# Two-layer hybrid encoder: weight halves three parts ahead, raw weights in three buffers, moves at three per part

## The chip, the core and the metric

The kernel runs on one core of a Trainium2 chip. The metric is the device time of one execution in microseconds (us). A core has a matrix engine (TensorE, PE in the profile; its weight loads are PEld), a vector engine (VectorE, DVE), a scalar engine (ScalarE, ACT), GpSimd (POOL) and SyncE (SP), which here only issues transfers from main memory. The engines run in parallel, each one in the order of its own queue, and wait for each other by semaphores. SBUF is the on-chip working memory; PSUM holds what PE sums up.

## The reference

The input is 256 tokens of 2048 channels, in float32. Each of two layers does this:

```python
h = rms_norm(x, norm_g)
u = jnp.einsum('bsd,de->bse', h, w_in)               # q, k, v, gate path of four mixers, merge gates
ya, yb, yc, yd = four attention mixers of u            # A, B, C, D; 4 heads of 128 each
y = jnp.stack([ya, yb, yc, yd], axis=2)
z = jnp.stack([az, bz, cz, dz], axis=2)
branch = jnp.einsum('bsnm,nmd->bsnd', y * jax.nn.silu(z), w_branch)
gate = jax.nn.sigmoid(gates.reshape(b, s, N_BRANCH, D_MODEL) + gate_b)
merged = jnp.sum(gate * branch, axis=2)
x = x + jnp.einsum('bsd,de->bse', merged, w_out)
```

and the output is a last `rms_norm` of `x`. All weights are float32.

## The kernel before

**Parts.** All weight matrices of both layers are one list of 640 tiles of 128 x 1024 float32 (512 KB each). What the program does with one tile is called a part here; `j` counts the parts. To keep float32 accuracy, a weight tile `raw` is split into two halves of a shorter format: `whi` is `raw` rounded (ACT, line 286), and `wlo` is `raw` minus `whi` (DVE, line 287). The activations are split in the same way. A part is 12 matmuls of 512 columns: for each of two row tiles of the weights and two blocks of 128 tokens, high by high, high by low and low by high (lines 213 to 215; `mm3`, `mm_m`). In the program's names the first and third line of each three read `whi`, the second reads `wlo`.

**Lookahead.** In part `j` the loop (from line 668) issues the load of tile `j + LD` (`LD` = 4, `dma_w`, line 112), splits tile `j + LS` (`LS` = 2, `split_w`, line 119) and issues the matmuls of tile `j`. There are four `raw` buffers and three each of `whi` and `wlo`. So the split of tile `j + 2` writes the buffers of tile `j - 1` and waits until PE has finished part `j - 1`; and a load waits until the tile that was in its buffer has been split, on ACT and on DVE. In the first parts the input `x` comes in eight pieces (`dma_x`, `h_tiles`), and the loads of weights 1 to 3 stand ahead of the loop, held back by small copies on POOL (`hold`).

**Units.** Parts form units: `M` (8 parts, one block of columns of the input projection), `G` (8 parts, a gate), `R` (2 parts, a branch projection) and `P` (8 parts, the output projection), in the order of `unit_list` (line 45). When a unit is done, its result is taken out of PSUM by DVE and ACT (`ev_M`, `ev_gate`, `ev_branch`, `ev_out`). PSUM has two buffers for units.

**Moves.** Results that the next product needs the other way round are turned (`turn`, line 300): one DVE transpose within 32 x 32 blocks (line 312), then 16 ACT copies that move the blocks (line 314, "moves" here), then a split into halves. The moves do not stand in one piece: they go to a list `post`, `step` of them in each following part, behind that part's split (`issue_after`, line 718). The step is 3 for most turns, 4 for branch D and 6 for the merged branches (`ev_branch`, for `x == "B"`, line 567) and for the second layer's input (`ev_out`, line 584). The order in a queue is made by a scheduler that sees these constraints, so two neighbouring groups of moves may end up side by side.

**Attention.** The attention of a branch is cut into steps `s1` to `s7` (line 406) that run in slots between the parts. `s5` splits the transposed probabilities of a head into `pth` and `ptl` (two buffers each), and `s6` multiplies them on PE.

**The end.** In the last unit (`alone`) the two blocks of tokens have PSUM buffers of their own. From `si >= 5` on only block 0 is multiplied at once; block 1's products of those parts (`late`) follow after the last part, so that block 0 can be finished and written out (`ev_last`) beside them.

Of the kernel before, what the change touches and what calls it, by code (L numbers as in the profile page):

```python
# [9 lines left out]
F32 = mybir.dt.float32  # L10
F32R = mybir.dt.float32r
# [6 lines left out]
P = 128  # L18
SEQ = 256
# [55 lines left out]
def encoder_kernel(ctx: ExitStack, tc: tile.TileContext, a: dict, out: bass.AP):  # L75
    nc = tc.nc
    LD = 4
    LS = 2
    NBUSY = 10

    const = ctx.enter_context(tc.tile_pool(name="const", bufs=1))
# [2 lines left out]
    wpool = ctx.enter_context(tc.tile_pool(name="wpool", bufs=4))  # L84
    wk = ctx.enter_context(tc.tile_pool(name="wk", bufs=2))
# [7 lines left out]
    def nm(s):  # L93
        uid[0] += 1
        return f"{s}_{uid[0]}"
# [8 lines left out]
    raw_q = {}  # L104
# [6 lines left out]

    def dma_w(j, after=None):
        if j < NSUB:
            t = wpool.tile([P, 1024], F32, tag="raw", name=nm("raw"))
            hold(t, after)
            nc.sync.dma_start(t, a["w"][j])
            raw_q[j] = t

    def split_w(j):
        if j < NSUB:  # L120
            raw = raw_q.pop(j)
            hi = wpool.tile([P, 1024], F32R, tag="whi", name=nm("whi"), bufs=3)
            lo = wpool.tile([P, 1024], F32R, tag="wlo", name=nm("wlo"), bufs=3)
            for c in (slice(0, 512), slice(512, 1024)) if j == 0 else (slice(0, 1024),):
                last = halves(raw[:, c], hi[:, c], lo[:, c])
            wstate[j] = (hi, lo)
            return last
        return None
# [5 lines left out]
    xT = {0: x0[:, NV:].rearrange("p (k t) -> p k t", k=2)}  # L134
    xm = [per.tile([P, 2, 512], F32, name=f"xm{n}") for n in range(4)]

    def dma_x(i, after=None):
        if 0 < i < 8:
            xT[i] = st()[:, 0:2, :]
            hold(xT[i][:, 0, :], after)  # L140
            nc.sync.dma_start(xT[i], a["x"][:, 2 * i:2 * i + 2, :])

    nc.sync.dma_start(x0, a["x0"])
    raw_q[0] = wpool.tile([P, 1024], F32, tag="raw", name=nm("raw"))
    for q in range(2):
        c = slice(q * 512, (q + 1) * 512)
        nc.sync.dma_start(raw_q[0][:, c], a["w"][0][:, c])
# [1 line left out]
    dma_x(1, raw_q[0][:, 0:1])  # L149
    dma_w(2, raw_q[0][:, 512:513])  # L150
    dma_x(2, raw_q[1][:, 0:1])
    dma_w(3, xT[1][:, 0, 0:1])
    assert LD == 4
    ones = const.tile([P, P], F32, name="ones")
    nc.vector.memset(ones, 1.0)
    warm = const.tile([P, 1], F32, name="warm")
# [163 lines left out]
    def turn_split(u, tmp, hi, lo, post, step=3):  # L320
        t = tmp.rearrange("p (h t) -> p h t", t=SEQ)
        turn(u, t, post, lambda: halves(t, hi, lo), step)
# [83 lines left out]
    def attn_slots(x, layer):  # L406
# [79 lines left out]
                nc.tensor.transpose(H[h][:, k, blk * P:(blk + 1) * P], it["p"][:, k * P:(k + 1) * P], ident)  # L486

        def s5(h):
            hi = wk.tile([P, 2, SEQ], F32R, tag="pth", name=nm("pth"))
            lo = wk.tile([P, 2, SEQ], F32R, tag="ptl", name=nm("ptl"))  # L490
            halves(H.pop(h), hi, lo)
            H[h] = hi, lo

# [60 lines left out]
    def ev_branch(x, n, ps, post):  # L554
        G = S.pop("G")
        if x == "A":
            S[f"m{n}"] = per.tile([P, 2, 512], F32, tag=f"m{n}", name=nm("m"))
        m = S[f"m{n}"]
        for blk in range(2):
            o = m if x == "A" else G  # L560
            nc.vector.tensor_tensor(o[:, blk, :], ps[:, blk, :], G[:, blk, :], op=ALU.mult)  # L561
        if x != "A":
            nc.vector.tensor_tensor(m, m, G, op=ALU.add)  # L563
        if x == "B":

            S[f"mh{n}"], S[f"ml{n}"] = st(F32R), st(F32R)
            turn_split(m, m.rearrange("p b m -> p (b m)"), S[f"mh{n}"], S[f"ml{n}"], post, 6)

    def ev_out(n, ps, post):

        nc.vector.tensor_tensor(xm[n], ps, xm[n], op=ALU.add)
        for blk in range(2):
            s = squares(F["ss"], n, blk)
        if n == 0:
            sqrt_table(s[:, 0:1])

        h_tile(n)
        t = wk.tile([P, 4, SEQ], F32, tag="u", name=nm("u"), bufs=1)

        def split():  # L580
            for c in range(4):
                h_split(1, 4 * n + c, t[:, c, :])

        turn(xm[n], t, post, split, 6)

    F = {}

# [44 lines left out]
    def h_tiles(i):  # L632
        if i < 8:
            for c in range(2):
                h_split(0, 2 * i + c, xT[i][:, c, :])
# [28 lines left out]
    for layer in range(DEPTH):  # L664
        final = layer + 1 == DEPTH
        units = unit_list(layer)
        opened = {}
        for ui, si in sub_list(layer):
            kind, name, i = units[ui]
            nsub = unit_subs(kind)  # L670
            alone = final and (kind, i) == ("P", 3)
            if si == 0:
                if kind == "G":
                    b = BR.index(name)
                    gb = wk.tile([P, 512], F32, tag="gb", name=nm("gb"), bufs=1)
                    if (layer, name, i) == (0, "A", 0):
                        hold(gb, xm[3][:, 0, 0:1])
                    nc.sync.dma_start(gb, a["gate_b"][layer, b:b + 1, i * 512:(i + 1) * 512].partition_broadcast(P))
                    S["gb"] = gb
                if name == "bk":  # L680
                    b_bias(layer)
                if (kind, i) == ("P", 0):
                    new_sums()
                    if final:
                        fin_start()
                ps = ps_main.tile([P, 2, 512], F32, tag="main", name=nm("ps"))
                outs = [(blk, ps[:, blk, :]) for blk in range(2)]
                if alone:
                    outs[1] = 1, ps_main.tile([P, 2, 512], F32, tag="main", name=nm("ps"))[:, 1, :]
                if kind == "R":  # L690
                    yh, yl = S[name + "yh"], S[name + "yl"]
                    sh, sl = (lambda k: yh[:, k, :]), (lambda k: yl[:, k, :])
                elif kind == "P":
                    sh, sl = (lambda k, h=h: S[f"m{h}{k // 4}"][:, k % 4, :] for h in "hl")
                else:
                    sh, sl = (lambda k, h=h: hs[k // 4][:, h, k % 4, :] for h in range(2))
                opened[ui] = ps, outs, sh, sl
            ps, outs, sh, sl = opened[ui]
            nk = 2 * nsub
            if (name, si) in (("akdk", 5), ("dq", 5)):  # L700
                d_tables(layer, int(name == "akdk"), None if layer or name == "dq" else xm[3][:, 0, 0:1])
            dma_x(j + LD - 1)
            dma_w(j + LD)
            h_tiles(j + LS - 1)
            behind = split_w(j + LS)
            if j in early:
                early[j]()
            if j == 11:
                layer_stats(0, F["ss"])
                ev_M(*held.pop())  # L710
            hi, lo = wstate.pop(j)
            half = alone and si >= 5
            mm_m(outs[:1] if half else outs, hi, lo, sh, sl, 2 * si, nk, j < 4)
            if half:
                late.append((hi, lo, si))
            with ExitStack() as order:
                for ins in behind or ():
                    order.enter_context(tc.issue_after(ins.ins))
                for f in post[:1]:
                    f()  # L720
                del post[:1]
                if si == nsub - 1:
                    if kind == "M" and "rc" not in S:
                        held.append((layer, name, ps, post))
                    elif kind == "M":
                        ev_M(layer, name, ps, post)
                    elif kind == "G":
                        ev_gate(layer, name, i, ps)
                    elif kind == "R":
                        ev_branch(name, i, ps, post)  # L730
                    elif not final:
                        ev_out(i, ps, post)
                        if i == 3:
                            layer_stats(1, F["ss"])
                    else:
                        ev_last(i, 0, outs[0][1])
                        for h, l, s in late:
                            mm_m(outs[1:], h, l, sh, sl, 2 * s, nk)
                        ev_last(i, 1, outs[1][1])
                    if kind == "M" and name[1:] == "z":  # L740
                        x = name[0].upper()
                        for k, s in enumerate(attn_slots(x, layer)):
                            side.append(s)
                            side.extend([] for _ in range(SPREAD[x][k % 2]))
                if side:
                    for fn, arg in side.pop(0):
                        fn(arg)
            j += 1
        assert final or not side
# [120 lines left out]
```

## Time and profile before

| what | value |
|---|---|
| median of 3 runs | 1863.76 us (1863.42 to 1864.97) |
| the profiled execution | 1864.2 us, of which the span of the profile is 1862.4 us |
| PE busy | 1833.5 us, 98% of the span |
| PEld busy | 1505.5 us, 81% |
| DVE busy | 1179.0 us, 63% |
| ACT busy | 1151.7 us, 62% |
| `wlo` split, DVE, x641 | 1220 ns each |
| `whi` split, ACT, x641 | 1058 ns each |
| loads of `raw`, x639 | 512 KB each, 3.9 us to landing (median) |
| DMA | 192 GB/s on average |

The span is cut into 40 slices on the page; PE shows 9 or more tenths in all but the last, and the clock granted to it is 9 tenths or more in all. The record of a 512-column matmul is about 0.39 us long, but the records overlap: a matmul starts before the record of the one before it ends. For what PE loses, the distance from start to start is therefore read, and not the busy share.

### The profile page before, as it was taken

The page shows a single profiled execution, that of the slowest core. Times are in us where ns is not written, and L with a number is a line of the kernel's source. Part 1 is how long each engine was busy: PE and PEld are TensorE (multiplying, and loading weights), DVE is VectorE, ACT ScalarE, POOL GpSimd, SP SyncE. Part 2 cuts the span into 40 slices and gives each one's busy share as a digit, 9 for nine tenths or more (in the row PEclk, how much of TensorE's full clock was granted, in tenths as well). Part 3 has the DMA queues.
Part 4 walks back from the last instruction along what each step waited for, and adds up shares of the span by engine and source line. Part 5 has one row for each costly group of instructions (what it writes and reads, how often), then busy time and mean ns, then how long its engine had stood idle before and what let it go on. Part 6 is the DMA issues. An engine that isn't in the chain of part 4 may idle for free.

```text
span 1862.4 us, 22697 instructions
## 1 busy us (share of the span) xinstructions
PE 1833.5 (98%) x8260; PEld 1505.5 (81%) x8260; DVE 1179.0 (63%) x1600; ACT 1151.7 (62%) x1712; POOL 5.1 (0%) x18
## 2 busy tenths in 40 slices
PE   9999999999999999999999999999999999999998
PEld 7888788888888888777888887888888888887776
DVE  6767566666665675665557675765666556755655
ACT  6676666556446764667767676655575457546663
POOL 1000000000000000000000000000000000000000
PEclk9999999999999999999999999999999999999999
DMA  8655555665576566655665555566655765565754
GB/s 310 203 184 181 180 178 188 198 196 175 183 208 204 180 189 195 197 186 174 190 204 186 177 172 180 175 207 198 196 175 175 220 198 178 189 199 180 222 190 148
DMA packets 110848, 356.94 MB, mean 192 GB/s; under 512 B 19984, under 2 KB 20496, under 8 KB 110736
## 3 DMA queue, kind: packets, MB, share of 16 engines
q1 hardware_dynamic: 110448, 354.98, 60.2%
q8 instruction: 64, 1.05, 0.2%
q10 hardware_dynamic: 288, 0.52, 0.1%
q14 instruction: 48, 0.39, 0.1%
HBM read 353.36 MB, written 2.10 MB: 191 GB/s over the span
## 4 chain that ended last, share of the span: by engine, by line
PE 84%; ACT 9%; DVE 4%; issue 2%; DMA 1%; POOL 0%; DVEq 0%; SPq 0%; ACTq 0%; POOLq 0%
PE ps L214 27%; PE ps L215 27%; PE ps L213 26%; ACT whi L286 2%; DVE wlo L287 2%; ACT u L314 2%; ACT m L314 2%; ACT st L314 1%; PE tp L486 1%; DVE T L312 1%; DVE m L563 0%; ACT dku L314 0%; DMA raw<-w 0%; PE y L214 0%; PE y L213 0%
## 5 line engine op out<-in xcount | busy, mean ns | idle before, releaser
L287 DVE TENSOR_TENSOR wlo<-raw,whi 128x1024 fp32r<-128x1024 f32 (+1 forms) x641 | 779.7, 1220 | 612.1 <-ACT whi L286 609.6
L286 ACT ACTIVATE whi<-raw 128x1024 fp32r<-128x1024 f32 (+1 forms) x641 | 676.4, 1058 | 606.7 <-PE ps L215 486.0
L214 PE MATMUL ps<-wlo,h 128*128 128x512 f32 x2032 | 794.9, 391 | 10.1 <-DVE wlo L287 9.3
L213 PE MATMUL ps<-whi,h 128*128 128x512 f32 x2032 | 794.5, 391 | 2.1 <-ACT whi L286 2.1
L215 PE MATMUL ps<-whi,h 128*128 128x512 f32 x2032 | 791.7, 390 | 0.0
L214 PEld LDWEIGHTS ps<-wlo,h 128*128 128x128 f32 x2032 | 381.7, 188 | 95.6 <-DVE wlo L287 20.7
L213 PEld LDWEIGHTS ps<-whi,h 128*128 128x128 f32 x2032 | 381.7, 188 | 82.4 <-ACT whi L286 5.5
L215 PEld LDWEIGHTS ps<-whi,h 128*128 128x128 f32 x2032 | 381.6, 188 | 78.8
L214 PE MATMUL ps<-wlo,st 128*128 128x512 f32 x512 | 200.8, 392 | 4.6 <-DVE wlo L287 4.6
L213 PE MATMUL ps<-whi,st 128*128 128x512 f32 x512 | 199.8, 391 | 2.2 <-ACT whi L286 2.2
L215 PE MATMUL ps<-whi,st 128*128 128x512 f32 x512 | 199.3, 389 | 0.0
L214 PEld LDWEIGHTS ps<-wlo,st 128*128 128x128 f32 x512 | 96.1, 188 | 28.4 <-DVE wlo L287 8.9
L213 PEld LDWEIGHTS ps<-whi,st 128*128 128x128 f32 x512 | 96.1, 188 | 24.0 <-ACT whi L286 3.9
L215 PEld LDWEIGHTS ps<-whi,st 128*128 128x128 f32 x512 | 96.2, 188 | 19.4
L314 ACT ACTIVATE st<-T 32x256 f32<-32x256 f32 x256 | 106.2, 415 | 7.8 <-DVE T L312 4.1
L314 ACT ACTIVATE u<-T 32x256 f32<-32x256 f32 (+1 forms) x224 | 89.5, 399 | 7.2 <-DVE T L312 4.3
L314 ACT ACTIVATE m<-T 32x256 f32<-32x256 f32 x128 | 53.2, 415 | 10.2 <-DVE T L312 8.7
L549 DVE SCALAR_TENSOR_TENSOR G<-ps,ry,gb 128x512 f32<-128x512 f32 x64 | 45.0, 745 | 12.9 <-PE ps L215 12.8
L551 ACT ACTIVATE G<-G 128x1024 f32<-128x1024 f32 x32 | 34.0, 1061 | 6.9 <-DVE G L549 6.8
L312 DVE STREAM_TRANSPOSE T<-u 128x1024 f32<-128x1024 f32 (+1 forms) x26 | 31.2, 1199 | 7.7 <-ACT dku L314 7.5
L561 DVE TENSOR_TENSOR G<-ps,G 128x512 f32<-128x512 f32 x48 | 30.9, 684 | 5.6 <-PE ps L215 5.6
L459 ACT ACTIVATE p<-p,ng 128x256 f32<-128x256 f32 (+1 forms) x48 | 27.6, 574 | 6.1 <-DVE ng L458 5.2
(141 smaller groups left out, 836.5 us busy)
## 6 DMA issues: line engine op xcount, KB each, us to landing
raw<-w SPq DMA_DIRECT2D x639, 512.0 KB, 3.9
gb<-gate_b SPq DMA_DIRECT2D x32, 256.0 KB, 4.4
xm<-xm SPq DMA_DIRECT2D x4, 512.0 KB, 8.9
st<-rpb SPq DMA_DIRECT2D x32, 64.0 KB, 4.2
st<-x SPq DMA_DIRECT2D x7, 256.0 KB, 6.2
dx<-tabx SPq DMA_DIRECT2D x4, 256.0 KB, 3.9
st<-fg SPq DMA_DIRECT2D x2, 512.0 KB, 5.3
out<-xm SPq DMA_DIRECT2D x4, 256.0 KB, 2.6
```

What stands on the lines that cost most here:

```text
L213: nc.tensor.matmul(o, ah, bh, start=start, stop=False)
L214: nc.tensor.matmul(o, ah, bl, start=False, stop=False)
L215: nc.tensor.matmul(o, al, bh, start=False, stop=stop)
L286: return (nc.scalar.activation(hi, u, AF.Copy), nc.vector.tensor_tensor(lo, u, f32(hi), op=ALU.subtract))
L287: nc.vector.tensor_tensor(lo, u, f32(hi), op=ALU.subtract))
L312: nc.vector.transpose(t, u)
L314: nc.scalar.activation(y[c:c + 32, :, :, a:a + 32], x[a:a + 32, :, :, c:c + 32], AF.Copy)
L459: nc.scalar.activation(p[:, 0:n], p[:, 0:n], AF.Exp, bias=ng, scale=1.0, accum_out=den)
L486: nc.tensor.transpose(H[h][:, k, blk * P:(blk + 1) * P], it["p"][:, k * P:(k + 1) * P], ident)
L549: nc.vector.scalar_tensor_tensor(G[:, blk, :], ps[:, blk, :], S["rc"][:, blk:blk + 1], gb, op0=ALU.mult, op1=ALU.add)
L551: nc.scalar.activation(G, G, AF.Sigmoid)
L561: nc.vector.tensor_tensor(o[:, blk, :], ps[:, blk, :], G[:, blk, :], op=ALU.mult)
```

## The change

- `LS` becomes 3: in part `j` tile `j + 3` is split; `whi` and `wlo` have four buffers each (the pool's default). The split of tile `j + 3` then again writes the buffers of tile `j - 1`.
- `raw` has three buffers in place of four. The load of tile `j + 4` writes the buffer of tile `j + 1`, which is split in part `j - 2`.
- In the first parts the older distances stay: for `j` below `EARLY` = 4 the loads run three parts ahead and the splits two; in part 4 two loads and two splits are issued. The load of weight 3 moves from ahead of the loop into part 0, behind the third piece of `x`.
- `pth` and `ptl` have one buffer each.
- The moves of the merged branches (`ev_branch`) and of the second layer's input (`ev_out`) go three to a part and not six, except for the last of four column blocks (`n == 3`).
- In the last unit block 1 is put off from `si >= 4` on and not from 5.

```diff
-    LS = 2
+    LS = 3
+    EARLY = 4
...
-            t = wpool.tile([P, 1024], F32, tag="raw", name=nm("raw"))
+            t = wpool.tile([P, 1024], F32, tag="raw", name=nm("raw"), bufs=3)
...
-            hi = wpool.tile([P, 1024], F32R, tag="whi", name=nm("whi"), bufs=3)
-            lo = wpool.tile([P, 1024], F32R, tag="wlo", name=nm("wlo"), bufs=3)
+            hi = wpool.tile([P, 1024], F32R, tag="whi", name=nm("whi"))
+            lo = wpool.tile([P, 1024], F32R, tag="wlo", name=nm("wlo"))
...
-    dma_w(3, xT[1][:, 0, 0:1])
...
-            hi = wk.tile([P, 2, SEQ], F32R, tag="pth", name=nm("pth"))
-            lo = wk.tile([P, 2, SEQ], F32R, tag="ptl", name=nm("ptl"))
+            hi = wk.tile([P, 2, SEQ], F32R, tag="pth", name=nm("pth"), bufs=1)
+            lo = wk.tile([P, 2, SEQ], F32R, tag="ptl", name=nm("ptl"), bufs=1)
...
-            turn_split(m, m.rearrange("p b m -> p (b m)"), S[f"mh{n}"], S[f"ml{n}"], post, 6)
+            turn_split(m, m.rearrange("p b m -> p (b m)"), S[f"mh{n}"], S[f"ml{n}"], post, 6 if n == 3 else 3)
...
-        turn(xm[n], t, post, split, 6)
+        turn(xm[n], t, post, split, 6 if n == 3 else 3)
...
-            dma_x(j + LD - 1)
-            dma_w(j + LD)
-            h_tiles(j + LS - 1)
-            behind = split_w(j + LS)
+            dma_x(j + 3)
+            h_tiles(j + 1)
+            for k in (1, 0) if j == EARLY else (j < EARLY,):
+                dma_w(j + LD - k, xT[1][:, 0, 0:1] if j == 0 else None)
+                behind = split_w(j + LS - k)
...
-            half = alone and si >= 5
+            half = alone and si >= 4
```

ACT's queue where the first merged branch of layer 0 is turned (`B0`, the `m` rows are the moves, `whi` the splits of weights, `st<-m` the split of the result), before:

```order
L286 ACTIVATE whi_6369<-raw_6315 128x1024
L314 ACTIVATE m_1894<-T_6338 32x8x32 x12
L286 ACTIVATE whi_6393<-raw_6342 128x1024
L314 ACTIVATE m_1894<-T_6338 32x8x32 x4
L286 ACTIVATE whi_6417<-raw_6367 128x1024
L286 ACTIVATE st_6336<-m_1894 128x1024
```

The same place after the change:

```order
L285 ACTIVATE whi_6370<-raw_6346 128x1024
L313 ACTIVATE m_1898<-T_6342 32x8x32 x6
L285 ACTIVATE whi_6391<-raw_6368 128x1024
L313 ACTIVATE m_1898<-T_6342 32x8x32 x3
L285 ACTIVATE whi_6412<-raw_6389 128x1024
L313 ACTIVATE m_1898<-T_6342 32x8x32 x3
L285 ACTIVATE whi_6433<-raw_6410 128x1024
L313 ACTIVATE m_1898<-T_6342 32x8x32 x3
L285 ACTIVATE whi_6454<-raw_6431 128x1024
L313 ACTIVATE m_1898<-T_6342 32x8x32
```

Twelve moves stood between two splits, and now at most six do; the 16 moves are spread over five gaps between splits, where they had two.

ACT's queue where branch D's k and q of layer 0 are turned (`dku` and `u` are the moves, `G` the gate's sigmoid), before:

```order
L286 ACTIVATE whi_1764<-raw_1716 128x1024
L314 ACTIVATE dku_543<-T_1654 32x4x32 x16
L286 ACTIVATE whi_1787<-raw_1738 128x1024
L286 ACTIVATE st_1653<-dku_543 128x512
L314 ACTIVATE u_1619<-T_1655 32x8x32 x8
L286 ACTIVATE whi_1809<-raw_1762 128x1024
```

And after:

```order
L285 ACTIVATE whi_1768<-raw_1742 128x1024
L313 ACTIVATE dku_547<-T_1658 32x4x32 x16
L285 ACTIVATE whi_1791<-raw_1766 128x1024
L285 ACTIVATE st_1657<-dku_547 128x512
L313 ACTIVATE u_1623<-T_1659 32x8x32 x8
L285 ACTIVATE whi_1813<-raw_1789 128x1024
```

The rows are the same ones in the same order; each `whi` in them is now the split of the tile that follows, so one more split has been done ahead of the moves.

SP's queue in the first parts (`st` the pieces of `x`, `raw` the weights 1 to 5), before:

```order
L116 DMA raw_92<-w 128x1024
L141 DMA st_95<-x 128x512
L116 DMA raw_98<-w 128x1024
L141 DMA st_101<-x 128x512
L116 DMA raw_104<-w 128x1024
L141 DMA st_149<-x 128x512
L116 DMA raw_151<-w 128x1024
L141 DMA st_174<-x 128x512
L116 DMA raw_176<-w 128x1024
```

And after:

```order
L117 DMA raw_92<-w 128x1024
L142 DMA st_95<-x 128x512
L117 DMA raw_98<-w 128x1024
L142 DMA st_101<-x 128x512
L142 DMA st_146<-x 128x512
L117 DMA raw_152<-w 128x1024
L142 DMA st_172<-x 128x512
L117 DMA raw_178<-w 128x1024
L142 DMA st_196<-x 128x512
```

The third piece of `x` now stands ahead of weight 3, and each weight after it has one more piece of `x` in front of it.

## Rows read from the trace of the kernel before

**Rows 1.** The page: the span, and its part 1.

```profile
span 1862.4 us, 22697 instructions
PE 1833.5 (98%) x8260; PEld 1505.5 (81%) x8260; DVE 1179.0 (63%) x1600; ACT 1151.7 (62%) x1712; POOL 5.1 (0%) x18
```

**Rows 2.** Timeline of PE at the first merge: start, length, instruction, [idle before].

```profile
764.27 0.39 PE L214 MATMUL ps<-wlo,h 128*128 128x512 f32 x1
764.50 0.39 PE L215 MATMUL ps<-whi,h 128*128 128x512 f32 x1
765.17 0.51 PE L213 MATMUL ps<-whi,h 128*128 128x512 f32 x1 [0.28 <-ACT whi L286]
766.43 0.50 PE L214 MATMUL ps<-wlo,h 128*128 128x512 f32 x1 [0.76 <-DVE wlo L287]
766.76 0.39 PE L215 MATMUL ps<-whi,h 128*128 128x512 f32 x1
```

**Rows 3.** Waits of PE from 40 to 1830 us: total, times, longest.

```profile
PE ps L214 <- DVE wlo L287: 13.4, 23, 0.8
PE ps L213 <- ACT whi L286: 4.3, 12, 0.8
```

**Rows 4.** Timeline of PE: a short delay without an idle time shown.

```profile
90.33 0.39 PE L213 MATMUL ps<-whi,h 128*128 128x512 f32 x1
90.83 0.50 PE L214 MATMUL ps<-wlo,h 128*128 128x512 f32 x1
```

**Rows 5.** Timeline of ACT at the first merge.

```profile
758.91 5.12 ACT L314 ACTIVATE m<-T 32x256 f32<-32x256 f32 x12 [1.09 <-DVE T L312]
764.06 1.06 ACT L286 ACTIVATE whi<-raw 128x1024 fp32r<-128x1024 f32 x1
765.14 1.69 ACT L314 ACTIVATE m<-T 32x256 f32<-32x256 f32 x4
```

**Rows 6.** Waits of PE from 170 to 206 us, branch D of layer 0.

```profile
PE ps L214 <- DVE wlo L287: 2.5, 4, 0.8
PE ps L213 <- ACT whi L286: 1.0, 2, 0.8
```

**Rows 7.** Busy time from 182.9 to 205.9 us: PE, PEld, DVE, ACT, POOL, clock, DMA.

```profile
182.90:205.90 23.00, 20.27 (x84) 15.09 (x83) 12.26 (x13) 22.42 (x44) 0.00 (x0) 1.00 0.45 149
```

**Rows 8.** Timeline of PE where the last of D's delays ends.

```profile
205.24 0.50 PE L214 MATMUL ps<-wlo,h 128*128 128x512 f32 x1 [0.77 <-DVE wlo L287]
```

**Rows 9.** Timeline of DVE ahead of D's moves.

```profile
175.15 2.35 DVE L287 TENSOR_TENSOR wlo<-raw,whi 128x1024 fp32r<-128x1024 f32 x2
...
181.66 0.70 DVE L312 STREAM_TRANSPOSE T<-dku 128x512 f32<-128x512 f32 x1
```

**Rows 10.** Timeline of ACT at the same place.

```profile
179.29 1.06 ACT L286 ACTIVATE whi<-raw 128x1024 fp32r<-128x1024 f32 x1 [0.92 <-PE ps L215]
182.01 1.06 ACT L286 ACTIVATE whi<-raw 128x1024 fp32r<-128x1024 f32 x1 [1.66 <-PE ps L215]
```

**Rows 11.** The view of line 116, the loads of raw weights: issue to landing.

```profile
DMA to landing us min/median/max: 3.1/3.9/9.0
```

**Rows 12.** Timeline of ACT in the first parts: the splits of weights 3 to 5.

```profile
14.49 1.06 ACT L286 ACTIVATE whi<-raw 128x1024 fp32r<-128x1024 f32 x1 [0.36 <-DMA raw<-w]
...
17.32 1.06 ACT L286 ACTIVATE whi<-raw 128x1024 fp32r<-128x1024 f32 x1 [0.44 <-DVE h L289]
...
19.28 1.06 ACT L286 ACTIVATE whi<-raw 128x1024 fp32r<-128x1024 f32 x1
```

**Rows 13.** Timeline of PE: the last delay of the first parts.

```profile
19.69 0.50 PE L214 MATMUL ps<-wlo,h 128*128 128x512 f32 x1 [0.47 <-DVE wlo L287]
```

**Rows 14.** Timeline of PE: the last product that reads a head's `pth`.

```profile
145.97 0.28 PE L215 MATMUL y<-pth,st 128*128 128x256 f32 x1
```

**Rows 15.** Timeline of ACT: the next write of `pth`.

```profile
150.69 0.57 ACT L286 ACTIVATE pth<-tp 128x512 fp32r<-128x512 f32 x1
```

**Rows 16.** Timeline of DVE at the end: block 0's last step, block 1's first.

```profile
1853.39 0.48 DVE L628 TENSOR_SCALAR xo<-xo,f 128x512 f32<-128x512 f32 x1
1854.22 0.69 DVE L602 TENSOR_TENSOR xm<-ps,xm 128x512 f32<-128x512 f32 x1 [0.34 <-PE ps L215]
```

More of the change, by code (lines that the diff above doesn't have):

```diff
@@ L143, in encoder_kernel @@
     nc.sync.dma_start(x0, a["x0"])
-    raw_q[0] = wpool.tile([P, 1024], F32, tag="raw", name=nm("raw"))
+    raw_q[0] = wpool.tile([P, 1024], F32, tag="raw", name=nm("raw"), bufs=3)
     for q in range(2):
@@ L151, in encoder_kernel @@
     dma_x(2, raw_q[1][:, 0:1])
-    dma_w(3, xT[1][:, 0, 0:1])
-    assert LD == 4
     ones = const.tile([P, P], F32, name="ones")
```

## The prediction

> **What bounds the kernel now.** I read the page's busy shares first: PE 98%, DVE 63%, ACT 62% [rows 1]. PE sets the end, and no edit takes work from PE, so the change can only win where PE waits. The second view is PE's timeline. In a steady stretch a 512-column matmul starts 0.23 us after the one before (764.27, 764.50), 0.2275 us on average over a part; a part of 12 is 2.73 us. At the first merge of branch B the starts are 764.50, 765.17, 766.43, 766.76: 2.26 us for three steps that take 0.68, so 1.58 us is lost, where the idle times shown add up to 1.04 us [rows 2]. The record of a matmul (0.39 us) hides 0.16 us of each wait, and the start behind the wait is late by another 0.11. So a wait that is shown as w costs w + 0.27.
>
> The third view is PE's waits between the start and the tail: 23 for `wlo` and 12 for `whi`, 17.7 us as shown [rows 3]; with 35 x 0.27 that is 27.2 us. Seven delays are too short for the list: at 90 us the step takes 0.50 us and not 0.23 [rows 4], with the late start behind it 0.38 us. The six others lie up to 1320 us and are alike; 2.6 us together. **So 29.8 us is lost because a weight half is late, 1.6% of the span.**
>
> The Trainium skill ("Perfetto Trace Analysis", Identifying the Most-Contended Engine) says that the busy share of matmuls tells little about the room that PE has, because pipelined matmuls overlap in the trace, and that the busy share of the weight loads is better. The trace agrees: by idle times the prize would be 17.7 us, by start times it is 29.8.
>
> Why are the halves late? They are made by ACT and then DVE two parts ahead, and ACT's queue has other work in front of them. At the first merge twelve moves take 5.12 us, and the split behind them starts at 764.06, when PE is already out of work [rows 5]. The lost time falls into groups: eight merges of branch B (four in each layer, the first shown) at 1.58 us, 12.6 us; branch D in each layer, six waits shown as 3.5 us [rows 6] and so 5.1 us, 10.2 us for both; the output projection of layer 0 and the single delays, the remaining 7.0 us.
>
> **The lookahead (LS 3, four `whi` and `wlo`).** The split of tile j + 3 waits for the same event as that of tile j + 2 did, the end of part j - 1, and stands at the same place in ACT's queue. So each half is ready at the time at which the half of the tile ahead of it was ready, which is one part, 2.73 us, more slack wherever ACT had caught up. A burst that now costs less than 2.73 us costs nothing. That covers each of B's merges (1.58), the output projection (its two neighbouring waits stay below 2) and the single delays: 12.6 + 7.0 = 19.6 us. Nothing is removed from ACT or DVE; the cover is their idle time between bursts, 38% of the span [rows 1].
>
> **Branch D is deeper.** ACT is busy for 22.42 of the 23.0 us from 182.9 on [rows 7]: it never waits there, so its chain stays where it is and PE cannot be faster than ACT's list. With no delay, PE would want the half that comes at 205.24 [rows 8] 5.1 us sooner, at 200.1; this place in the list now serves the part that follows, so 202.9. It is still 2.4 us late. A second piece comes from the three `raw` buffers. The split at 179.29 [rows 10] will use a buffer that is only given back when the first of the two `wlo` from 175.15 ends, at 176.4 [rows 9]; with a landing of 3.9 us [rows 11], and 4.6 us in this stretch as an estimate between the median and the maximum, it cannot start before 181.0, 1.7 us later than now. DVE's turn of `dku` stands behind that tile's `wlo` (181.66 [rows 9]); ACT's moves, behind the split at 182.01, take up some of it, so I put 1.0 us on the chain. **3.4 us remain for each layer, 6.8 us in all;** bounds are 0 (the whole burst is covered) and 10.2 (all stays).
>
> **Moves at three to a part.** The same 16 moves (0.42 us each, 1.69 for four [rows 5]) lie between more splits: three moves and a split are 1.28 + 1.06 = 2.3 us, less than the 2.73 of a part, where six and a split were 3.6. At B's merges and the output projection this alone would remove most of the delay. With the lookahead it is a second cover for the same 19.6 us and is counted at nothing. Block n = 3 keeps six: its 1.58 us lie within 2.73, with 1.15 to spare. The results are ready about three parts later and are read more than eight parts later (at n below 3): nothing waits.
>
> **Three `raw` buffers: an added wait.** The load of tile j + 4 waits for the `wlo` of tile j + 1, made in part j - 2. From there the split that reads it is three parts away, 8.2 us. The loop is landing 3.9 + split 2.4 (1.06 on ACT, 1.2 on DVE, their gaps) + issue 0.1 = 6.4 us for three parts, 2.1 us a part: faster than PE's 2.73, with 1.8 us to spare. It would set the pace only from landings of 5.7 us on. Behind the waiting load on SP stand the next gate rows and the pieces of bias; they are read most of a unit later, so nobody waits for them. Where the load is late, ACT's queue stands behind a split; up to 1.7 us (above) is less than the slack won. Counted in D alone; for the 19.6 us the bounds are 0 and a third given back, 6.5.
>
> **First parts.** The third piece of x goes ahead of weight 3, and the weights come one piece later. The spacing of the splits of weights 4 and 5, 17.32 and 19.28 [rows 12], is 1.96 us for a weight and a piece, 768 KB; the piece alone is a third, 0.65 us. PE's last early delay waits for the `wlo` of weight 4 [rows 13], so 0.65 us is **lost**; bounds 0 (x's halves, now earlier, make it good) and 1.3 (twice).
>
> **The rest.** One buffer for `pth`: its last reader ends at 146.25 [rows 14] and the next write is at 150.69 [rows 15], 4.4 us later; no wait, and if the cover went, ACT would stand for part of a part. Putting off block 1 by one more part: PE's work and end are the same; block 0's last DVE step ends at 1853.87, and DVE then waits 0.34 us for block 1 [rows 16], so an earlier block 0 gives nothing; bounds 0 and 0.5 of gain, if its outputs' transfers slow those of block 1.
>
> **Sum.** 29.8 - 6.8 - 0.65 = 22.3 us. The profiled execution is 1864.2 us (span 1862.4 and 1.8 around it): 1841.9. The median is 0.4 us below the profiled one: **1841.5 us**.
>
> **Rivals.** *All of it goes.* If D's chain gets ahead early enough, the whole 29.8 us go: 1864.2 - 29.8 = 1834.4. For it: ACT idles 0.92 and 1.66 us just ahead of the burst [rows 10], because a buffer is missing; against it: the chain behind that has no gap [rows 7]. The Trainium skill ("Perfetto Trace Analysis", Optimization Strategy) says that the same gap repeating on the engine that should be full can mean that there are too few buffers; by that rule one more buffer ends all the gaps, which is this case. The trace bears it out at B, not at D.
>
> *More stays.* Late loads hold ACT's queue behind bursts, D keeps all its 10.2 us and a third of the other 19.6 comes back: gain 29.8 - 10.2 - 6.5 - 0.65 = 12.4, so 1851.8. For it: landings of up to 9.0 us exist [rows 11]; against: the median is far from the 5.7 that matter.
>
> *Slower: the loads set the pace.* With three buffers a part cannot be shorter than a third of landing + 2.5 us. At a mean landing of 5.9 us it is 2.80 us, 0.07 more than PE's; over 600 parts 42 us are lost and 22 won: about 1884. It is slower than before from a mean landing of 5.8 us on. Against it: the median of 3.9.
>
> *It does not do what it says.* If the scheduler put the moves ahead of the extra split, nothing would change: 1864. The queues of the changed kernel show the split ahead of D's moves and B's moves spread.
>
> **How the numbers follow.** Forecast (1838 to 1846) 0.50; all goes (1833 to 1838) 0.20; more stays (1846 to 1860) 0.20; no change 0.04; slower 0.06. Faster by over 0.2% (3.7 us, about what a measurement of this kernel can tell from no change): the first three, 0.90; same 0.04; slower 0.06. The range from 1833.5 to 1852 holds the first two, and the third up to its own time; about 0.2 is left out.
>
> **What would show it.** In the profile after: no PE wait for `whi` or `wlo` at the eight merges and in the output projection; at D one or two waits left, 2 to 4 us a layer by start times, with ACT without a gap through it; the last early delay of PE near 20.3 us; PE's step 0.2275 as now; the tail from the last matmul to the end as now, 8.2 us. Wrong would be: D's waits gone or whole, new waits of PE in the attention stretches, or `whi` waiting for loads over most of the run.

## The result, and the profile after

The changed kernel takes 1838.88 us (median of 4, 1838.11 to 1840.32), the kernel before 1864.37 in the same set (1863.42 to 1865.92). The ratio is 0.9863 with a 95% interval of 0.9846 to 0.9880: faster by 25.5 us, 1.4%. The profiled execution took 1840.32 us, the slowest of the four; its span is 1838.5 us, 23.9 less than before [rows 1].

The page after, span and part 1, and then the waits of PE from 40 to 1810 us (total, times, longest), which answer to [rows 3]:

```profile
span 1838.5 us, 22705 instructions
PE 1821.0 (99%) x8260; PEld 1509.1 (82%) x8260; DVE 1178.4 (64%) x1600; ACT 1153.9 (63%) x1712; POOL 4.1 (0%) x18
```

```profile
PE ps L212 <- DVE G L548: 2.8, 2, 1.4
PE ps L213 <- DVE wlo L286: 1.4, 2, 0.8
PE tp L485 <- DVE p L477: 0.3, 1, 0.3
```

The 35 waits for weight halves are down to two, and DVE and ACT are as busy as before [rows 1]. In their place stands one kind that the kernel before did not have: twice the first matmul of a unit waits until DVE has taken the result of a gate unit (`G`) out of the PSUM buffer that the new unit needs. At the first merge ACT's queue now reads as follows (start, length, instruction, idle before); [rows 5] are the same place before:

```profile
756.79 2.56 ACT L313 ACTIVATE m<-T 32x256 f32<-32x256 f32 x6 [0.71 <-DVE T L311]
759.37 1.06 ACT L285 ACTIVATE whi<-raw 128x1024 fp32r<-128x1024 f32 x1
760.46 1.27 ACT L313 ACTIVATE m<-T 32x256 f32<-32x256 f32 x3
761.75 1.06 ACT L285 ACTIVATE whi<-raw 128x1024 fp32r<-128x1024 f32 x1
```

From 740 to 960 us, the four merges and the output projection of layer 0, PE has no wait at all. What is left lies in branch D, here in layer 0. First PE, then DVE, then ACT ahead of the burst:

```profile
196.02 0.39 PE L212 MATMUL ps<-whi,st 128*128 128x512 f32 x1
197.01 0.50 PE L213 MATMUL ps<-wlo,st 128*128 128x512 f32 x1 [0.60 <-DVE wlo L286]
...
199.43 0.39 PE L214 MATMUL ps<-whi,st 128*128 128x512 f32 x1
201.22 0.47 PE L212 MATMUL ps<-whi,h 128*128 128x512 f32 x1 [1.40 <-DVE G L548]
```

```profile
198.53 1.23 DVE L286 TENSOR_TENSOR wlo<-raw,whi 128x1024 fp32r<-128x1024 f32 x1 [1.57 <-ACT whi L285]
199.67 1.40 DVE L548 SCALAR_TENSOR_TENSOR G<-ps,ry,gb 128x512 f32<-128x512 f32 x2
```

```profile
181.59 1.06 ACT L285 ACTIVATE whi<-raw 128x1024 fp32r<-128x1024 f32 x1 [1.53 <-DMA raw<-w]
183.65 1.06 ACT L285 ACTIVATE whi<-raw 128x1024 fp32r<-128x1024 f32 x1 [0.99 <-DMA raw<-w]
184.62 5.09 ACT L313 ACTIVATE dku<-T 32x128 f32<-32x128 f32 x16
```

By start times the `wlo` wait costs 0.87 us with the late start behind it and the `G` wait 1.56 (199.43 to 201.22, less a step of 0.23). The `G` that releases PE is DVE's next instruction behind a `wlo` that itself had stood 1.57 us waiting for ACT: ACT is late, and through DVE's queue now also holds PSUM. Layer 1 is alike (1.14 and 1.59).

The first parts got longer. ACT's and PE's rows, then busy time, clock and DMA share in two stretches (PE, PEld, DVE, ACT, POOL, clock, DMA share, GB/s):

```profile
16.81 1.06 ACT L285 ACTIVATE whi<-raw 128x1024 fp32r<-128x1024 f32 x1 [0.44 <-DMA raw<-w]
```

```profile
17.92 2.07 PE L224 MATMUL ps<-whi,h 128*128 128x512 f32 x4 [2.38 <-ACT whi L285]
```

```profile
18.00:21.00 3.00, 3.00 (x7) 2.39 (x8) 3.00 (x4) 2.84 (x6) 0.18 (x1) 0.50 0.74 244
21.00:24.00 3.00, 3.00 (x14) 2.43 (x13) 3.00 (x7) 2.60 (x4) 0.26 (x1) 0.98 0.96 333
```

Weight 3, now behind the third piece of `x`, is split at 16.81 and not at 14.49 [rows 12]. PE stands 2.38 us for it, and in the next 3 us its granted clock is 0.50, the lower of its two levels: 7 matmuls where the stretch behind has 14. The third matmul of part 4 starts at 22.72; before, it started at 20.03. So 2.7 us are lost here.

The account of the span, by PE's start times:

| piece | lost before | foreseen after | found after |
|---|---|---|---|
| B's merges, output projection, single delays | 19.6 | 0 | 0 |
| branch D, both layers | 10.2 | 6.8 | 5.2 |
| first parts, against before | | 0.65 | 2.7 |
| a PE wait for `p` at 1031.4 us | 0 | 0 | 0.4 |
| start of the last matmul to the end | 8.62 | same | 8.45 |

19.6 + 5.0 - 2.7 - 0.4 + 0.2 = 21.7 us, and the span gained 23.9. The other 2.2 us lie in steps too short to count as delays. From 40 us on, 512-column matmuls that start less than 0.30 us apart are 0.2274 us apart on average before and 0.2271 after, and there are some 7500 such steps. In a stretch without waits the step is 0.2267 in both; the first ten steps behind a wait take 0.230 on average in the kernel before. So each wait costs a little more than the 0.27 us that the prediction adds to it.

### The profile page after: what moved, and what is told of

It reads as the page before. It is cut to its first block, busy times and chain, and to the rows that moved or that the text cites. A ratio compares the mean times of both kernels' runs of the same rounds, so it can differ in the third digit from the quotient of the medians.

```text
span 1838.5 us, 22705 instructions
## 1 busy us (share of the span) xinstructions
PE 1821.0 (99%) x8260; PEld 1509.1 (82%) x8260; DVE 1178.4 (64%) x1600; ACT 1153.9 (63%) x1712; POOL 4.1 (0%) x18
## 4 chain that ended last, share of the span: by engine, by line
PE 89%; ACT 4%; DMA 3%; DVE 2%; issue 1%; SPq 0%; DVEq 0%; POOL 0%; ACTq 0%; POOLq 0%
PE ps L212 29%; PE ps L214 29%; PE ps L213 28%; DMA raw<-w 3%; ACT u L313 1%; ACT whi L285 1%; DVE wlo L286 1%; PE tp L485 1%; ACT dku L313 0%; PE y L213 0%; PE y L214 0%; PE y L212 0%; PE sc L416 0%; ACT st L313 0%; PE sc L214 0%
```

## Experiments

Each ratio is to the kernel before on the same chip, with its 95% interval.

**Only the moves at three.** The kernel before, with these edits in `ev_branch` and `ev_out`:

```diff
-            turn_split(m, m.rearrange("p b m -> p (b m)"), S[f"mh{n}"], S[f"ml{n}"], post, 6)
+            turn_split(m, m.rearrange("p b m -> p (b m)"), S[f"mh{n}"], S[f"ml{n}"], post, 6 if n == 3 else 3)
...
-        turn(xm[n], t, post, split, 6)
+        turn(xm[n], t, post, split, 6 if n == 3 else 3)
```

> The kernel before with one edit: the moves of the merged branches and of the second layer's input go three to a part, except in block n = 3. Lookahead two, four raw buffers, as before. Theory (each half is late because a burst stands in front of it; spreading the moves and looking further ahead are two covers for the same delay): the delays at the merges of n = 0 to 2 go (6 x 1.58 = 9.5 us) and most of the output projection's (about 3); branch D's 10.2 us, the merges of n = 3 (3.2) and the single delays (about 3) stay. About 1864.4 - 12.5 = 1852 us. Rival (the moves are what matters, the lookahead adds little): 1842 or less, with no delay at D either.

Measured: 1851.02 us, 0.9929 (0.9916 to 0.9941). PE's waits from 40 to 1815 us:

```profile
PE ps L214 <- DVE wlo L287: 6.6, 12, 0.8
PE ps L213 <- ACT whi L286: 2.4, 5, 0.8
```

17 of 35 waits are left, in D, at n = 3 and single ones. The moves alone are worth 13.2 us, half of the gain; the theory's time was 1852, and the rival's (1842 or less) did not come.

**All but the moves.** The changed kernel with these two lines as they were before; the second reads

```diff
-        turn(xm[n], t, post, split, 6 if n == 3 else 3)
+        turn(xm[n], t, post, split, 6)
```

> The changed kernel with one part undone: all moves at six to a part again. Theory: the lookahead of three alone covers bursts below 2.73 us, so the merges (1.58) and the output projection (below 2) show no wait of PE and the time is that of the changed kernel within 1.5 us, 1838 to 1841 us. Rival (both are needed, since late loads eat part of the lookahead behind a burst of twelve moves): waits at the merges come back, with 0.5 to 1.5 us each, 1843 to 1851 us.

Measured: 1851.71 us, 0.9930 (0.9917 to 0.9942), 12.8 more than the changed kernel (the executions range from 1848.42 to 1853.96). My theory, that one part of lookahead covers each burst of 1.58 us, fell; the rival, late loads behind a burst, is what the trace shows. ACT's waits from 740 to 960 us, PE's in the same stretch, and ACT's queue behind the first merge:

```profile
ACT whi L285 <- DMA raw<-w: 45.1, 32, 4.2
```

```profile
PE ps L213 <- DVE wlo L286: 2.2, 5, 0.8
PE ps L214 <- DVE st L286: 0.6, 1, 0.6
PE ps L212 <- ACT whi L285: 0.4, 1, 0.4
```

```profile
766.47 2.16 ACT L285 ACTIVATE whi<-raw 128x1024 fp32r<-128x1024 f32 x2
770.40 1.06 ACT L285 ACTIVATE whi<-raw 128x1024 fp32r<-128x1024 f32 x1 [1.77 <-DMA raw<-w]
772.57 1.06 ACT L285 ACTIVATE whi<-raw 128x1024 fp32r<-128x1024 f32 x1 [1.11 <-DMA raw<-w]
```

The first merge costs PE nothing, but it uses up the slack, the time from the end of a `wlo` to the matmul that first reads it. Here are the last `wlo` ahead of the twelve moves and the first behind them, each with its reader, at the first merge and at the third:

```profile
756.50 1.18 DVE L286 TENSOR_TENSOR wlo<-raw,whi 128x1024 fp32r<-128x1024 f32 x1
762.65 0.39 PE L213 MATMUL ps<-wlo,h 128*128 128x512 f32 x1
762.85 1.23 DVE L286 TENSOR_TENSOR wlo<-raw,whi 128x1024 fp32r<-128x1024 f32 x1 [5.17 <-ACT whi L285]
765.37 0.39 PE L213 MATMUL ps<-wlo,h 128*128 128x512 f32 x1
...
812.52 1.18 DVE L286 TENSOR_TENSOR wlo<-raw,whi 128x1024 fp32r<-128x1024 f32 x1
817.13 0.39 PE L213 MATMUL ps<-wlo,h 128*128 128x512 f32 x1
818.87 1.23 DVE L286 TENSOR_TENSOR wlo<-raw,whi 128x1024 fp32r<-128x1024 f32 x1 [5.16 <-ACT whi L285]
820.15 0.50 PE L213 MATMUL ps<-wlo,h 128*128 128x512 f32 x1
```

Some parts ahead of the first merge the slack is 5.87 us; it is 4.97 just before the moves, and 1.3 and then 1.2 behind them. Then each split waits for its raw weight, and the splits come 2.17 us apart, PE's parts 2.72. That is at best 0.55 us of slack won back per part, and less where the queue has other work. Ten parts later, just before the moves of the second merge, it is 3.55 and not 4.97, and that merge leaves 0.1. The third finds 3.42, and PE waits. In the kernel before, the splits in this stretch had waited for PE to give a half back, and none for a load:

```profile
ACT whi L286 <- PE ps L215: 53.9, 40, 1.7
```

So the loads in three buffers set the pace at which slack returns.

**Three raw buffers or four.** If that is the cause, a fourth `raw` buffer must end it with the moves still at six. To make room, one `p` buffer and one `t2` buffer go, working tiles of the attention and of the evictions (for `t2` one of three equal edits is shown, for `raw` and `p` one of two):

```diff
-            t = wpool.tile([P, 1024], F32, tag="raw", name=nm("raw"), bufs=3)
+            t = wpool.tile([P, 1024], F32, tag="raw", name=nm("raw"))
...
-        s = wk.tile([P, 512], F32, tag="t2", name=nm("sq"))
+        s = wk.tile([P, 512], F32, tag="t2", name=nm("sq"), bufs=1)
...
-            p = wk.tile([P, 512], F32, tag="p", name=nm("p"), bufs=3)
+            p = wk.tile([P, 512], F32, tag="p", name=nm("p"), bufs=2)
```

> The kernel of the run with all moves at six, with four raw buffers in place of three (to make room, the attention's p tile has two buffers and not three, and the squares' t2 one and not two). Theory (with all moves at six the lead of the weight halves falls by 4.7 us at a merge, from 5.9, and is refilled by only 0.3 to 0.6 us a part, because each split then waits for its load: three raw buffers limit the refill, and the next merge comes before the lead is back): ACT no longer waits for loads behind a merge, the lead is back at 5.8 us before each merge, at most 1 us of waits of PE is left at merges and output projection, and the time is 1838 to 1842 us. Rival (the bursts of twelve moves are too long for a lookahead of three in any case): the waits stay, 1849 to 1852 us.

Measured: 1842.61 us, 0.9885 (0.9870 to 0.9900), 9.1 less than with three. The same place in ACT's queue, and PE's waits from 40 to 1815 us:

```profile
766.52 2.94 ACT L285 ACTIVATE whi<-raw 128x1024 fp32r<-128x1024 f32 x3
770.83 1.06 ACT L285 ACTIVATE whi<-raw 128x1024 fp32r<-128x1024 f32 x1 [1.37 <-PE ps L214]
773.55 1.07 ACT L285 ACTIVATE whi<-raw 128x1024 fp32r<-128x1024 f32 x1 [1.66 <-PE ps L214]
```

```profile
PE ps L212 <- DVE G L548: 6.3, 2, 3.4
```

ACT catches up in one go (three splits side by side) and then waits for PE again; the slack is back at 5.87 us ahead of each merge, and no PE wait for a half is left anywhere. So lookahead with four raw buffers covers all merges without the moves; with three it needs them. What is left is D, where PE waits for PSUM for 3.1 and 3.5 us, and a clock at 0.50 behind the wait (columns as above):

```profile
199.50:202.50 3.00, 2.98 (x7) 2.43 (x8) 2.36 (x2) 2.97 (x4) 0.00 (x0) 0.50 0.78 266
```

D is worse here than in the changed kernel, and ACT's and DVE's queues show where (layer 0; layer 1 is alike):

```profile
190.61 5.10 ACT L313 ACTIVATE u<-T 32x256 f32<-32x256 f32 x12
196.83 1.22 DVE L286 TENSOR_TENSOR wlo<-raw,whi 128x1024 fp32r<-128x1024 f32 x1 [4.74 <-ACT whi L285]
```

Twelve moves stand in one piece, where the changed kernel has eight, and the `G` that frees PSUM is DVE's next instruction behind this `wlo`. The moves at six are not the reason: with them and three raw buffers the queue has eight, and PE's waits for `G` are the 2.8 us in 2 of the changed kernel. Whether the fourth buffer or the two that went changed the order was not tried.

**Only three raw buffers.** The kernel before with `bufs=3` for `raw`; the load then has to stand behind the split that frees its buffer (that of weight 3, ahead of the loop, likewise behind the split of weight 1):

```diff
-            dma_w(j + LD)
             h_tiles(j + LS - 1)
             behind = split_w(j + LS)
+            dma_w(j + LD)
```

> The kernel before with three raw buffers and not four, the load of tile j + 4 behind the split of tile j + 2; lookahead two, moves at six. Theory (three buffers only matter for the refill behind a burst, and with a lookahead of two the lead to be refilled is 3.1 us, for which ten parts suffice): PE's waits at the merges are 1.58 us each as before, and the time is that of before within 3 us, 1862 to 1867 us. Rival (three buffers cost by themselves, at every late load): 1870 us or more.

Measured: 1864.87 us, 1.0006 (0.9996 to 1.0015): no difference. ACT does wait for loads, and PE's waits hardly move (740 to 960 us; before the two PE groups were 5.1 in 9 and 1.1 in 4):

```profile
ACT whi L284 <- DMA raw<-w: 22.6, 14, 3.6
```

```profile
PE ps L212 <- DVE wlo L285: 6.2, 9, 0.8
PE ps L211 <- ACT whi L284: 1.1, 4, 0.3
```

With two parts of lookahead there is little slack to win back, so the pace of winning it back costs nothing. The price of the third buffer shows only together with the lookahead that it is meant to serve.

**One buffer for the probability halves.** The kernel before with `bufs=1` for `pth` and `ptl`.

> The kernel before with one edit: one buffer each for pth and ptl. Theory (the last reader ends 3.8 us or more before the next write): no wait, the time of before within 1.5 us. Rival (the scheduler's order or ACT's queue waits for it): 1867 us or more, with waits of ACT for PE in front of pth.

Measured: 1864.54 us, 1.0002 (0.9992 to 1.0011). Nothing, as foreseen.

**Weight 3 ahead of the third piece of x.** The changed kernel with

```diff
     split_w(1)
+    dma_w(3, xT[1][:, 0, 0:1])
...
-                dma_w(j + LD - k, xT[1][:, 0, 0:1] if j == 0 else None)
+                if j:
+                    dma_w(j + LD - k)
```

> The changed kernel with one part undone: the load of weight 3 stands ahead of the loop again and so ahead of the third piece of x; its buffer (three raw buffers) is free when tile 0 is split. Theory (the changed kernel loses 2.7 us in the first parts because weight 3 lands at 16.7 us and not at 14.4, so that PE stands for 2.4 us and its granted clock falls for 3 us): weight 3 lands near 14.4, no fall of the clock, the steady run of PE begins 2 us earlier, 1836.5 to 1837 us. Rival (the three raw buffers themselves starve the first parts): weight 3 or 4 lands as late, less than 0.7 us won.

Measured: 1838.05 us, 0.9856 (0.9841 to 0.9872). The early rows are back at the old times:

```profile
14.40 1.06 ACT L285 ACTIVATE whi<-raw 128x1024 fp32r<-128x1024 f32 x1 [0.36 <-DMA raw<-w]
```

```profile
19.90 0.50 PE L213 MATMUL ps<-wlo,h 128*128 128x512 f32 x1 [0.77 <-DVE wlo L286]
```

The third matmul of part 4 starts at 20.23, 2.5 us earlier than in the profiled execution after, but the medians differ by 0.8 only, too little to be told apart, and the theory's 1836.5 to 1837 did not come. The loss is not in every execution: with the changed order of the loads the profiled executions of three other kernels (moves at six with three and with four raw buffers, and D's moves on DVE) have this matmul at 21.89, 20.24 and 19.85. With weight 3 first, six profiled executions have it between 19.71 and 20.26. So late starts (two of four) were seen with the changed order alone; in the median they cost less than 1 us.

**Half of D's moves on DVE.** In the changed kernel, the moves of D's k and q with odd block rows become copies on DVE (`dve` is set for branch D alone):

```diff
-                nc.scalar.activation(y[c:c + 32, :, :, a:a + 32], x[a:a + 32, :, :, c:c + 32], AF.Copy)
+                o, i = y[c:c + 32, :, :, a:a + 32], x[a:a + 32, :, :, c:c + 32]
+                if dve and a % 64:
+                    nc.vector.tensor_copy(o, i)
+                else:
+                    nc.scalar.activation(o, i, AF.Copy)
```

> The changed kernel with half of branch D's moves (8 of 16 for k, 8 of 16 for q, in each layer) on DVE in place of ACT, some 5.8 us less on ACT in each D burst. Theory (what is left at D, 2.4 us in layer 0 and 2.7 in layer 1, is ACT's list without a gap): the waits go in both layers, 5.2 us, about 1834 us. Rival (part of what is left, 1.6 us a layer, is PE's wait for PSUM, which DVE frees behind its own queue, and DVE has more work now): 3 us or more stay, 1836.5 us or above.

Measured: 1832.65 us, 0.9830 (0.9817 to 0.9844), the fastest of all and 6.2 below the changed kernel. PE's waits from 40 to 1815 us, and D's burst of layer 0 in the changed kernel and in this one (columns as above):

```profile
PE ps L212 <- DVE G L552: 0.3, 1, 0.3
```

```profile
182.90:205.90 23.00, 20.99 (x92) 16.76 (x91) 11.86 (x13) 21.75 (x43) 0.00 (x0) 1.00 0.52 171
```

```profile
182.90:205.90 23.00, 23.00 (x104) 19.02 (x103) 18.90 (x26) 17.36 (x26) 0.00 (x0) 1.00 0.61 204
```

ACT has 5.6 us of idle time in this stretch where it had 1.25, PE does 104 matmuls and not 92, and the wait for PSUM has gone with the one for `wlo`, but for 0.3 us in layer 1. (This execution is 2.9 us ahead here, since its first parts were not late; from 180.0 to 203.0 us ACT's idle time is 5.15 and PE does 103.) That supports the reading above: PSUM was held because ACT's list was late, not because DVE had too much to do. DVE is given 8 copies for each turn and releases PSUM in time.

**Both last edits together.** Weight 3 first, and half of D's moves on DVE.

> The changed kernel with both improvements: weight 3 ahead of the third piece of x, and half of branch D's moves on DVE. Theory (the first parts' loss, 0.6 to 2.7 us from one execution to another, and D's 4.7 us are separate and add up): no wait of PE above 1 us at any place behind the first 15 us, 1831 to 1833 us, with executions closer together than the changed kernel's. Rival (the first parts' loss is already absent in most executions of the kernel with D's moves on DVE): no difference to that one, 1832.7 us.

Measured: 1833.10 us, 0.9834 (0.9819 to 0.9848): no difference from the moves on DVE alone, as the rival had it. With the early loss not in the median, there is nothing to take from it. Putting block 1 off from `si` 4 on was not tried by itself. The last matmul of the changed kernel starts 8.45 us ahead of the end and not 8.62; but three kernels that still put it off from 5 on (only the moves, only three raw buffers, one buffer for the halves) have 8.46. So no run shows that this edit gives the 0.2 us.

## Why the prediction was right, and where it was not

**Right in the time.** 1841.5 us was foreseen with a range of 1833.5 to 1852, and 1838.88 came. The sum of the steps was 22.3 us; the span gained 23.9. That they lie so close is in part chance: D gave 1.6 us more than foreseen and the short steps 2.2 that were not counted, and the first parts of this execution took 2.05 more and the wait for `p` 0.4. Four steps stand: what PE loses is read from start to start (the waits shown add up to 17.7 us before and 4.5 after, and yet the span gained 23.9); the 19.6 us outside D go; D does not go, since ACT's list there has no gap; one buffer for `pth` is free.

**The step that failed: "the moves are a second cover, counted at nothing".** I took one part of lookahead to be a full cover for each burst of 1.58 us, as though each burst came upon fresh slack. It covers the first only. The numbers that decide it stood in my own paragraph on the three raw buffers: the loop takes 2.1 us a part (2.17 measured) against PE's 2.73 (2.72 measured). I read "faster than PE" as "costs nothing" and did not ask how long 0.6 us a part (0.55 measured) takes to rebuild what a burst uses up, 4.7 us at the first merge: eight parts and more, with ten parts between merges and other work in them. So both covers are needed with three buffers: without the moves 12.8 us come back, twice the 6.5 that I gave as the bound for late loads. Moves at three keep a burst small, and then the slow refill is enough. The sum came out right because the change has both.

The Trainium skill ("Perfetto Trace Analysis", Optimization Strategy) says that the same gap repeating on the engine that should be full can mean too few buffers. The runs agree at the merges: the fourth raw buffer takes ACT's waits for loads in 740 to 960 us from 45.1 us to none and ends all of PE's. They do not at D, where PE still waits 6.3 us with that buffer, and 0.3 in the kernel with three raw buffers and less work on ACT.

**Mis-sized terms.** D: 6.8 foreseen, 5.2 found. The raw-load piece was right in kind and place (the split not before 181.0, found 181.59 behind a wait for its load; the moves start at 184.62 and not at 182.98, with PE 0.65 us later at this place, so 1.0 later against PE). But I looked for the next late thing among the halves only: over half of what is left, 1.6 us a layer, is the wait for PSUM, which the view of DVE's queue behind the late `wlo` could have shown. First parts: 0.65 foreseen with a bound of 1.3, found 2.7 in the profiled execution, since the clock fell behind the wait; in the median it is near the 0.8 that weight 3 first gives back, or nothing. The tail: 0 foreseen, 0.2 found, inside its bound, and found too where the edit was left out.

**The rivals.** "All goes" named 1834.4 and D's chain getting ahead; the buffers tried did not do that, taking work from ACT did, at 1832.65. "More stays" had the right mechanism (late loads hold ACT behind bursts) and would have been the result, 1851.71, without the moves. That this is its 1851.8 is chance: there D loses 5.5 us by start times and not 10.2, and the rest more than a third of 19.6. "Slower, the loads set the pace" fell: the landings stay at 3.9 us in the median (3.0 to 8.0), and ACT's 68 waits for a load over the whole run, 84.0 us, lie mostly in slack (the view of line 117, who waited for it):

```profile
  ACT whi L285: 84.0, 68
```

## What to carry to other kernels

A lookahead is a store that each burst empties: its worth is the depth only for the first burst, and behind it the pace at which the stage ahead of it refills it, so divide what a burst takes by (consumer's time for a part minus producer's) and compare with the parts between bursts. Where one engine's list has no gap, more lookahead takes only a part (at D 10.2 us became 5.2), and moving work to a neighbour can take the rest (one wait of 0.3 us is left). When a late instruction leaves the path, look along its engine's queue for what stands behind it: here the release of PSUM behind a late `wlo`.

## What the hardware showed that I had not expected

A short stop of PE in an otherwise full run can cost more than itself: behind waits of 2.4 us (first parts after the change) and 3.1 us (D, moves at six with four raw buffers) the granted clock is 0.50, 1.2 GHz, for about 3 us, in which 7 matmuls run and not 13 or 14. The length of the wait does not settle it. Behind the 1.6 us of the changed kernel's D the clock stays at 1.00 over the stretch; and in D of layer 0 the kernel before and the one with one buffer for the probability halves have the same waits ahead of 196 us, none shown above 0.8 us, and then run so, the kernel before first:

```profile
196.00:199.00 3.00, 3.00 (x15) 2.33 (x14) 2.12 (x3) 2.92 (x6) 0.00 (x0) 1.00 0.54 178
196.00:199.00 3.00, 3.00 (x9) 2.32 (x8) 2.18 (x3) 2.92 (x6) 0.00 (x0) 0.50 0.55 178
```

No run here shows what decides it; the medians of these two kernels are alike (ratio 1.0002).

The start of the first parts is not fixed by the order of the loads either: the third matmul of part 4 starts between 19.85 and 22.72 us in executions that have the same order; no run here shows why.
